# Stick-breaking attention as a sum over differenced values, and half of its gates as paired half-size products

## The chip, the cores and the metric

The kernel runs on one core of a Trainium2 chip. The metric is the device time of one execution in microseconds. TensorE (PE) does the matrix products and the transposes, VectorE (DVE), ScalarE (ACT) and GpSimd (POOL) the elementwise work, and SyncE (SP) issues all the DMAs that matter here, in order, from one queue. Weight loads of TensorE have a row of their own in the profile, PEld.

## The reference, cut to what matters

One layer of a decoder: `h = RMSNorm(x)`, one input projection of `h`, a gated linear attention branch (GLA, 4 heads), a stick-breaking branch (8 heads of width 128), learned merge gates, and an output projection. T = D = 1024. The part that the change rewrites:

```python
z = q @ k.T * scale                      # per head, 128 queries against their causal prefix
log1m = where(causal, log_sigmoid(-z), 0)
between = cumsum(log1m, reverse=True) - log1m
A = where(causal, exp(log_sigmoid(z) + between), 0)
o_sb = A @ v                             # then times silu(s_gate), then @ w_pb
```

So the weight of key s for query t is beta[t,s] times the product of (1 - beta[t,j]) over the keys j between s and t.

## The kernel before

Every matrix product is done in float32r with operands split into a high and a low part, hi and lo, and three matmuls (hi*hi, hi*lo, lo*hi). A split is one ACT copy (L165) and one DVE subtraction (L166). The stages, in order:

- **Norm and first values.** `x` is normed, transposed and split. The products in token-major form (`proj_n`, L223) give the stick-breaking values of heads 0 and 1 together with the rank-16 decay code, and then the values of the other heads (`vjobs`, `v_unit`). They need no transpose: the tokens already lie on the partitions. `store_v` writes them to DRAM (`d_v`).
- **Pairs.** Most other projections are done 256 columns at a time by `pair_job`, a Strassen-Winograd scheme: 7 units, each a product of half size (12 matmuls of 128x512, L270 to L272), in place of 8. Its weights need four sums on POOL (L244 to L247) and seven split halves. A list, `Pairs([...])`, sets the order of 28 pairs: merge gates, GLA values (`gv_pair`, which transposes its result on PE, L605), GLA q, k and gates, stick-breaking q and k, merge gates. Units run one by one between other work: 22 beside the GLA decay, some beside jobs that load and sum weights for later (`tjobs`), `GLA_AT` = 56 units in all before GLA begins, and then 4 for each block of GLA.
- **Stick-breaking.** 8 heads times 8 query blocks are 64 steps. Step s issues `scores` for step s+2, then filler, then `turn` for step s. `scores` does the z products (L956 to L958), one or two pieces in two PSUM banks; on each piece ACT makes two sigmoids, of -z into `eb` (L960) and of z into `be` (L961); DVE runs a scan of products over the whole row of `eb` (L964); POOL puts zeros into the last 128 columns of `be` above the diagonal (L965); DVE multiplies `be` by the shifted scan (L968). `turn` transposes the 1 to 8 blocks of `be` on PE (L980) and splits them into `ath`, `atl` (the four blocks of the same half) and `afh`, `afl` (the four far blocks). `values` (matmuls L1001 to L1003 into `av`) runs twice per head, after the turns of step 0 (second half of the head before) and step 4, multiplies by the gate (L1004) and stores `d_osb`.
- **Filler.** The eight stick-breaking gates (L204 to L206, 24 matmuls of 128x512 in a unit, two units for each head, then SiLU) and the GLA output projection run as single units between these steps. `SB_PLAN` says how many units stand before and after the turn of each of a head's steps: one at step 3, one at step 6, one after step 7. Two units run before the loop and six after it.
- **q loads.** `load_q` (L903) loads the queries of two steps at a time into one of two buffers, in turn; the load for steps 4 and 5 of a head goes into the buffer that steps 0 and 1 read, so it can start only when the z product of step 1 has read it.
- **Output.** Both projections of the stick-breaking output and of the merged result, again as pairs of half-size products, then the residual and the norm.

From GLA to the end of stick-breaking the order on every engine comes from the framework's scheduler, which works on the order in which the code is written; each engine then runs its own list in order.

## Time and profile before

| | us |
|---|---|
| three runs | 1201.83, 1204.47, 1204.98; median 1204.47 |
| the profiled execution, its own time | 1205.73 |
| its span, first to last instruction | 1204.0 |
| norm and first values (0 to 115) | 115 |
| pairs beside decay, weight sums and GLA (115 to 727) | 612 |
| stick-breaking with filler (727 to 1015) | 288 |
| output (1015 to 1204) | 189 |

The times of stages are read off the span by where their lines first appear. In a busy row, overlapping matmuls count once; the start of one matmul to the start of the next is the rate at which PE works.

### The profile page before, as it was taken

Reading aid. Unit: us, or ns where it says so; the run is one execution under the profiler, and the core shown is the slowest. Engines: PE = TensorE matmul, PEld = TensorE weight load, DVE = VectorE, ACT = ScalarE, POOL = GpSimd, SP = SyncE. Lnnn points to the kernel's source line nnn. Section 1 sums busy time; section 2 is a strip of 40 time slices with the busy share of each in tenths; the row PEclk is TensorE's granted clock in tenths of the full one; section 3 lists DMA queues with packets and bytes.
Section 4 is the critical chain, followed back from the end, with each engine's and each line's share of the span. In section 5 each row is a group of like instructions: output and inputs, shape, how many; then the busy total and the mean of one; then the engine's idle time right before and its main releaser. Section 6 shows DMA issues by size and latency. Waiting matters only on the chain.

```text
span 1204.0 us, 17310 instructions
## 1 busy us (share of the span) xinstructions
PE 1185.2 (98%) x6087; PEld 997.8 (83%) x6087; DVE 855.4 (71%) x1341; ACT 555.8 (46%) x1081; POOL 316.7 (26%) x303
## 2 busy tenths in 40 slices
PE   8999999999999999999999999999999999999997
PEld 8999878888888888888888887888878888788886
DVE  5475876896676676776674646777787775578986
ACT  5343763334334444444443425445455553365543
POOL 1486513243322322422323201111021110700001
PEclk9999999999999999999999999999999999999999
DMA  7545349988546646666655267564788547758652
GB/s 282 182 140 154 136 164 337 338 303 265 185 145 197 179 157 210 209 200 204 218 172 166 80 230 259 168 209 159 251 263 304 169 131 242 254 161 282 225 192 105
DMA packets 207090, 247.67 MB, mean 206 GB/s; under 512 B 12662, under 2 KB 141708, under 8 KB 205468
## 3 DMA queue, kind: packets, MB, share of 16 engines
q1 hardware_dynamic: 206428, 245.52, 62.3%
q8 instruction: 48, 0.79, 0.3%
q10 hardware_dynamic: 576, 1.05, 0.2%
q14 instruction: 38, 0.31, 0.1%
HBM read 154.25 MB, written 92.27 MB: 205 GB/s over the span
## 4 chain that ended last, share of the span: by engine, by line
PE 83%; DVE 7%; DMA 3%; ACT 3%; issue 3%; SPq 1%; POOL 0%; DVEq 0%; ACTq 0%
PE pp L270 12%; PE pp L272 12%; PE pp L271 12%; PE pp L223 8%; PE pp L204 4%; PE pp L206 4%; PE pp L205 4%; PE av L1002 2%; PE av L1003 1%; PE z L956 1%; PE av L1001 1%; PE tr L980 1%; PE xb L1368 1%; PE xb L1367 1%; PE z L957 1%
## 5 line engine op out<-in xcount | busy, mean ns | idle before, releaser
L166 DVE TENSOR_TENSOR wl<-tt,wh 128x1024 fp32r<-128x1024 f32 x56 | 70.6, 1261 | 49.6 <-ACT wh L165 49.4
L965 POOL TENSOR_SCALAR_AFFINE_SELECT be<-be 128x128 f32<-128x128 f32 x64 | 38.0, 595 | 236.7 <-ACT be L961 218.3
L309 DVE TENSOR_TENSOR f<-pp,f 128x512 f32<-128x512 f32 x84 | 57.8, 688 | 59.1 <-PE pp L272 55.7
L964 DVE TENSOR_TENSOR_SCAN eb<-eb,m 128x128 f32<-128x128 f32 (+3 forms) x64 | 86.7, 1356 | 9.7 <-ACT eb L960 9.5
L165 ACT ACTIVATE wh<-tt 128x1024 fp32r<-128x1024 f32 x56 | 59.3, 1059 | 67.2 <-PE pp L271 63.8
L244 POOL TENSOR_TENSOR tt<-raw 128x512 f32<-128x512 f32 x28 | 39.5, 1412 | 190.9 <-DVE wl L166 184.2
L165 ACT ACTIVATE wh<-raw 128x1024 fp32r<-128x1024 f32 x47 | 49.7, 1059 | 81.0 <-PE pp L271 39.1
L276 ACT ACTIVATE f<-pp 128x512 f32<-128x512 f32 x84 | 49.7, 592 | 79.9 <-PE pp L272 79.9
L166 DVE TENSOR_TENSOR wl<-raw,wh 128x1024 fp32r<-128x1024 f32 x47 | 70.5, 1501 | 22.4 <-ACT wh L165 21.6
L231 POOL TENSOR_TENSOR r<-r,nhalf 128x1 f32<-128x1 f32 x40 | 24.2, 604 | 193.2 <-DVE r L230 182.7
L960 ACT ACTIVATE eb<-z 128x384 f32<-128x384 f32 (+4 forms) x96 | 48.8, 508 | 43.4 <-issue 22.8
L968 DVE TENSOR_TENSOR be<-be,eb 128x128 f32<-128x128 f32 (+3 forms) x64 | 48.3, 757 | 3.6
L961 ACT ACTIVATE be<-z 128x384 f32<-128x384 f32 (+4 forms) x96 | 49.2, 513 | 0.0
L270 PE MATMUL pp<-ha22h,wh 128*128 128x512 f32 x112 | 44.7, 399 | 0.3 <-DVE f L309 0.2
L270 PE MATMUL pp<-ha11h,wh 128*128 128x512 f32 x112 | 44.5, 397 | 0.0
L270 PE MATMUL pp<-ha12h,wh 128*128 128x512 f32 x112 | 44.5, 397 | 0.0
L270 PE MATMUL pp<-S1h,wh 128*128 128x512 f32 x112 | 44.4, 396 | 0.0
L270 PE MATMUL pp<-S3h,wh 128*128 128x512 f32 x112 | 44.1, 394 | 0.0
L270 PE MATMUL pp<-S2h,wh 128*128 128x512 f32 x112 | 44.0, 392 | 0.0
L270 PE MATMUL pp<-S4h,dh 128*128 128x512 f32 x112 | 43.9, 392 | 0.0
L271 PE MATMUL pp<-ha22l,wh 128*128 128x512 f32 x112 | 43.7, 390 | 0.0
L272 PE MATMUL pp<-ha22h,wl 128*128 128x512 f32 x112 | 43.7, 390 | 0.0
(519 smaller groups left out, 3979.7 us busy)
## 6 DMA issues: line engine op xcount, KB each, us to landing
raw<-in_w_in_dram SPq DMA_DIRECT2D x31, 1024.0 KB, 6.5
d_v<-o SPq DMA_DIRECT2D x32, 256.0 KB, 3.0
d_gv<-o SPq DMA_DIRECT2D x32, 256.0 KB, 4.0
d_t<-t SPq DMA_DIRECT2D x16, 512.0 KB, 4.7
v<-d_gv SPq DMA_DIRECT2D x32, 256.0 KB, 3.5
d_ogl<-o SPq DMA_DIRECT2D x64, 128.0 KB, 2.8
d_q<-o SPq DMA_DIRECT2D x16, 512.0 KB, 5.2
d_k<-o SPq DMA_DIRECT2D x16, 512.0 KB, 3.4
```

What stands on the lines that cost most here:

```text
L165: nc.scalar.activation(hi, src, AF.Copy)
L166: eng.tensor_sub(lo, src, hi.bitcast(F32))
L223: nc.tensor.matmul(pt[:, 0:n], *ops[kb][i], start=k == 0, stop=k == 3 * KB - 1)
L270: nc.tensor.matmul(pt, bh[:, j], ah[:, j], start=first and j == 0, stop=False, skip_group_check=True)
L271: nc.tensor.matmul(pt, bh[:, j], al[:, j], start=False, stop=False, skip_group_check=True)
L272: nc.tensor.matmul(pt, bl[:, j], ah[:, j], start=False, stop=j == 3, skip_group_check=True)
L276: nc.scalar.activation(t[nm], t[bank], AF.Copy)
L309: nc.vector.tensor_add(add, bank, add)
L960: nc.scalar.activation(om[:, osl], zt[:, 0:w], AF.Sigmoid, scale=-inv_sqrt)
L961: nc.scalar.activation(be[:, osl], zt[:, 0:w], AF.Sigmoid, scale=inv_sqrt)
L964: nc.vector.tensor_tensor_scan(rest, rest, m1[:, off:T][:, ::-1], 1.0, op0=ALU.mult, op1=ALU.max)
L968: nc.vector.tensor_mul(be[:, off:T], be[:, off:T], om[:, off + 1:T + 1])
```

## The change

- The values are summed by parts. With C[t,s] the product of (1 - beta[t,j]) over j from s to t-1, the weight of key s is C[t,s+1] - C[t,s]. So the output is a sum over C[t,s] times (v[s-1] - v[s]), with -v[0] for s = 0, plus the last value row of the query block's prefix (there the masked part of the scan is 1 and the differences telescope). The scan's own output is transposed: the second sigmoid, POOL's mask and the DVE product are gone. `be` now names the scan's buffer.
- The stick-breaking values must be differenced along tokens, so they move to pairs (`sv_pair`, d-major, tokens along the free axis): `vend` keeps every 128th value column (a [128,4] copy), `diff` subtracts neighbours (a [128,511] subtraction and one column), and the result is transposed on PE, split and stored. The GLA values take their place in the token-major form.
- `values` adds `vend` and multiplies by the gate in four instructions of 128 columns in place of one of 512. It stands earlier than the turn of step 2 (second half of the head before) and of step 5.
- The gates of heads 0 to 3 become two pairs (`sg_pair`), so there are 30 pairs; 70 units in place of 56 run before GLA, and the jobs beside them start every 5 units, not every 3. Eight gate units leave the stick-breaking filler; `SB_PLAN` has one unit at step 3 and one at step 6.

```diff
-SB_PLAN = [(0, 0), (0, 0), (0, 0), (1, 0), (0, 0), (0, 0), (1, 0), (0, 1)]
+SB_PLAN = [0, 0, 0, 1, 0, 0, 1, 0]
-GLA_AT = 56
+GLA_AT = 70
...
+    def sg_pair(i):
+        return pair_job(w_in, C_SG + i * DV,
+                        lambda J, n, bank, add: silu(total(bank, add), d_sg[2 * i + J][:, half(n)]))
+    def sv_pair(i):
+        held = []
...
+            h = 2 * i + J
+            nc.vector.tensor_copy(vend[:, h, 4 * n:4 * n + 4], add[:, P - 1:HALF:P])
+            held.append((J, n, h, add))
+            if (J, n) != (1, 1):
+                while held:
+                    diff(*held.pop())
+        def diff(J, n, h, add):
+            d = ev.tile([P, HALF], F32, tag="f", name="f")
+            nc.vector.tensor_sub(d[:, 1:HALF], add[:, 0:HALF - 1], add[:, 1:HALF])
+            if n:
+                nc.vector.tensor_sub(d[:, 0:1], vend[:, h, 3:4], add[:, 0:1])
+            else:
+                nc.vector.tensor_scalar(d[:, 0:1], add[:, 0:1], -1.0, None, op0=ALU.mult)
...
-                  [gv_pair(0)] + gla_qk(0) + [gg_pair(0), gv_pair(1), gg_pair(1)] + gla_qk(1) +
-                  [gv_pair(2), gg_pair(2), gv_pair(3), gg_pair(3)] +
-                  [f for i in range(4) for f in (qk_pair(C_SQ, i, d_q), qk_pair(C_SK, i, d_k))] +
-                  [merge_pair(C_MB, i, d_gb) for i in range(4)] + [merge_pair(C_MA, 3, d_ga)], late)
+                  gla_qk(0) + [gg_pair(0), gg_pair(1)] + gla_qk(1) + [gg_pair(2), gg_pair(3)] +
+                  [f for i in range(4) for f in (qk_pair(C_SQ, i, d_q), sv_pair(i), qk_pair(C_SK, i, d_k))] +
+                  [sg_pair(i) for i in range(2)] + [merge_pair(C_MB, i, d_gb) for i in range(4)] + [merge_pair(C_MA, 3, d_ga)], late)
...
-            nc.scalar.activation(om[:, osl], zt[:, 0:w], AF.Sigmoid, scale=-inv_sqrt)
-            nc.scalar.activation(be[:, osl], zt[:, 0:w], AF.Sigmoid, scale=inv_sqrt)
+            nc.scalar.activation(om[:, off + pc * w:off + (pc + 1) * w], zt[:, 0:w], AF.Sigmoid, scale=-inv_sqrt)
...
-        nc.gpsimd.affine_select(be[:, T - P:T], be[:, T - P:T], pattern=[[-1, P]],
-        nc.vector.tensor_mul(be[:, off:T], be[:, off:T], om[:, off + 1:T + 1])
...
-        nc.vector.tensor_mul(gate, pav, gate)
+        for q in range(4):
+            cs = slice(q * P, (q + 1) * P)
+            nc.vector.scalar_tensor_tensor(gate[:, cs], pav[:, cs], vend[:, h, 4 * g + q:4 * g + q + 1], gate[:, cs],
+                                           op0=ALU.add, op1=ALU.mult)
...
-        st.run(SB_PLAN[i][0])
+        st.run(SB_PLAN[i])
+        if i == 2 and h:
+            values(h - 1, 1)
+        elif i == 5:
+            values(h, 0)
         turn(h, i)
-        st.run(SB_PLAN[i][1])
-        if i % 4 == 0 and s:
-            values(*((h, 0) if i else (h - 1, 1)))
```

The order on the engines changes with it. First PE at the passage from head 0 to head 1, in the kernel before: the last `values` matmuls, the rest of step 3's z product, the turn of step 1 and the first z product of step 4 (128x320):

```order
L1001 MATMUL av<-ath,v 128x256
L1002 MATMUL av<-atl,v 128x256
L1003 MATMUL av<-ath,v 128x256
L957 MATMUL z<-k,q 128x512
L958 MATMUL z<-k,q 128x512
L980 MATMUL tr<-ident,be 128x128 x2
L956 MATMUL z<-k,q 128x320
```

The same passage in the changed kernel, from the turn of step 7 that follows the z product of step 1, to the first z product of step 4:

```order
L988 MATMUL tr<-ident,be 128x128 x4
L988 MATMUL pp<-ident,be 128x128 x4
L970 MATMUL z<-k,q 128x384
L971 MATMUL z<-k,q 128x384
L972 MATMUL z<-k,q 128x384
L988 MATMUL tr<-ident,be 128x128
L970 MATMUL z<-k,q 128x512
L971 MATMUL z<-k,q 128x512
L972 MATMUL z<-k,q 128x512
L1009 MATMUL av<-afh,v 128x512
L988 MATMUL tr<-ident,be 128x128 x2
L970 MATMUL z<-k,q 128x320
```

A filler unit and a whole `values` stood between the z products of steps 1 and 4; now the unit is gone and all of `values` but one matmul stands behind.

Second, DVE inside a pair whose result is transposed. Before, the end of `gv_pair(2)`: a total (`f<-pp,f`), a weight split of the next pair (`dl`, `wl`), and the low parts of the transposed result (`o<-tr,o`):

```order
L309 TENSOR_TENSOR f<-pp,f 128x512
L166 TENSOR_TENSOR dl<-raw,dh 128x512
L166 TENSOR_TENSOR o<-tr,o 128x512
L166 TENSOR_TENSOR wl<-tt,wh 128x1024
L166 TENSOR_TENSOR o<-tr,o 128x512 x2
```

Now the end of the first `sv_pair`, units 4 to 6:

```order
L609 COPY vend<-f 128x4
L308 TENSOR_TENSOR f<-pp,f 128x512
L165 TENSOR_TENSOR dl<-raw,dh 128x512
L609 COPY vend<-f 128x4
L617 TENSOR_TENSOR f<-f 128x511
L621 TENSOR_SCALAR f<-f 128x1
L617 TENSOR_TENSOR f<-f 128x511
L619 TENSOR_TENSOR f<-vend,f 128x1
L165 TENSOR_TENSOR wl<-tt,wh 128x1024
```

Two differences with their edge columns now stand between a total and the transposes that read them, and two results are transposed together (`tr<-ident,f` x8 on PE).

## Rows read from the trace of the kernel before

**Rows 1.** Page, part 1: busy time, share, instructions; part 2: granted clock

```profile
PE 1185.2 (98%) x6087; PEld 997.8 (83%) x6087; DVE 855.4 (71%) x1341; ACT 555.8 (46%) x1081; POOL 316.7 (26%) x303
PEclk9999999999999999999999999999999999999999
```

**Rows 2.** Windows: stretch, busy us of PE, PEld, DVE, ACT, POOL, clock, DMA share, GB/s

```profile
115.00:265.00 150.00, 149.49 (x669) 121.92 (x668) 117.81 (x128) 74.48 (x95) 54.37 (x35) 1.00 0.73 248
265.00:727.00 462.00, 462.00 (x2285) 380.42 (x2284) 305.02 (x627) 199.19 (x419) 135.23 (x130) 1.00 0.61 191
727.00:1015.00 288.00, 282.51 (x1481) 238.75 (x1480) 217.54 (x280) 145.16 (x330) 38.05 (x64) 1.00 0.64 210
```

**Rows 3.** Timeline of PE inside a gate unit: start us, duration us, line, operation

```profile
822.89 0.39 PE L206 MATMUL pp<-ha21h,wl 128*128 128x512 f32 x1
823.12 0.39 PE L204 MATMUL pp<-ha22h,wh 128*128 128x512 f32 x1
823.34 0.39 PE L205 MATMUL pp<-ha22l,wh 128*128 128x512 f32 x1
823.57 0.39 PE L206 MATMUL pp<-ha22h,wl 128*128 128x512 f32 x1
```

**Rows 4.** Waits 727 to 1015, PE and PEld: total us, times, longest us

```profile
PE av L1002 <- DVE atl L166: 3.1, 3, 1.5
PE z L956 <- ACT be L961: 1.6, 4, 0.7
PE pp L980 <- DVE be L968: 0.4, 1, 0.4
PE tr L980 <- DVE be L968: 0.3, 1, 0.3
...
PEld z L956 <- ACT be L961: 6.8, 17, 1.0
PEld av L1002 <- DVE atl L166: 4.5, 5, 1.8
PEld tr L980 <- DVE be L968: 1.0, 2, 0.7
```

**Rows 5.** Groups by line, 727 to 1015: busy us, mean ns, idle before

```profile
L968 DVE TENSOR_TENSOR be<-be,eb 128x128 f32<-128x128 f32 (+3 forms) x64 | 48.3, 757 | 3.6
L1004 DVE TENSOR_TENSOR f<-av,f 128x512 f32<-128x512 f32 x16 | 11.0, 686 | 17.0 <-PE av L1003 17.0
L570 DVE TENSOR_TENSOR o<-pp,o 128x512 f32<-128x512 f32 x15 | 10.3, 687 | 11.0 <-ACT o L569 6.3 <-DMA raw<-in_w_in_dram 4.8
L166 DVE TENSOR_TENSOR wl<-raw,wh 128x1024 fp32r<-128x1024 f32 x13 | 15.9, 1224 | 15.1 <-ACT wh L165 14.9
...
L961 ACT ACTIVATE be<-z 128x384 f32<-128x384 f32 (+4 forms) x96 | 49.2, 513 | 0.0
```

**Rows 6.** Groups by line and shape, whole span: the nearest to the new DVE work

```profile
L309 DVE TENSOR_TENSOR f<-pp,f 128x512 f32<-128x512 f32 x84 | 57.8, 688 | 59.1 <-PE pp L272 55.7 <-issue 2.1 <-PE tr L854 1.0
L166 DVE TENSOR_TENSOR o<-f,o 128x512 fp32r<-128x512 f32 x24 | 19.6, 816 | 4.7 <-ACT o L165 4.1
L166 DVE TENSOR_TENSOR dl<-raw,dh 128x512 fp32r<-128x512 f32 x28 | 20.2, 722 | 5.3 <-ACT dh L165 5.3
L857 DVE SCALAR_TENSOR_TENSOR g<-tr,vcol,g 128x128 f32<-128x128 f32 x64 | 19.4, 344 | 20.1 <-PE tr L854 20.1
L230 DVE TENSOR_SCALAR r<-ssq 128x1 f32<-128x1 f32 x40 | 5.8, 146 | 6.8 <-ACT xs L389 6.1 <-ACT on L844 0.7
```

**Rows 7.** Timeline of PE at a passage between heads, step 1's z to step 4's

```profile
826.16 0.28 PE L958 MATMUL z<-k,q 128*128 128x256 f32 x1
826.28 0.60 PE L980 MATMUL tr<-ident,be 128*128 128x128 f32 x4
826.72 0.60 PE L980 MATMUL pp<-ident,be 128*128 128x128 f32 x4
827.08 0.42 PE L956 MATMUL z<-k,q 128*128 128x384 f32 x1
827.34 0.33 PE L957 MATMUL z<-k,q 128*128 128x384 f32 x1
827.50 0.34 PE L958 MATMUL z<-k,q 128*128 128x384 f32 x1
...
839.35 0.39 PE L956 MATMUL z<-k,q 128*128 128x320 f32 x1
```

**Rows 8.** Timeline of SP there, and the tile q, 727 to 1015: landing

```profile
820.61 0.42 SPq L893 DMA_DIRECT2D k<-d_k  x1
826.48 0.52 SPq L903 DMA_DIRECT2D q<-d_q  x1
...
DMA to landing us min/median/max: 3.0/3.6/6.5
```

More of the change, by code (lines that the diff above doesn't have):

```diff
@@ L346, in hybrid_layer @@
     vst = {}
+    vend = const.tile([P, SB_H, NT], F32, tag="vend", name="vend")
     def store_v(key, i, tb):
-        st = vst.pop((key, tb // 2)) if tb % 2 else None
-        if st is not None:
-            for e in range(2):
-                nc.sync.dma_start(d_v[2 * i + e][:, tb - 1:tb + 1], st[:, :, :, e * P:(e + 1) * P].bitcast(F32))
+        if tb % 2:
+            nc.sync.dma_start(d_gv[i][:, tb - 1:tb + 1], vst.pop((key, tb // 2)).bitcast(F32))
     def v_stage(key, tb):
@@ L379, in load_vr @@
             rows = w_in[4 * i * P:(4 * i + 4) * P, :]
-            nc.sync.dma_start(raw[:, :, 0:DV], rows[:, C_SV:C_SV + DV].rearrange("(k p) c -> p k c", p=P))
+            nc.sync.dma_start(raw[:, :, 0:DV], rows[:, C_GV:C_GV + DV].rearrange("(k p) c -> p k c", p=P))
             nc.sync.dma_start(raw[:, :, DV:VR], rows[:, C_GR:C_GR + RANK].rearrange("(k p) c -> p k c", p=P))
@@ L482, in hybrid_layer @@
     ebl = const.tile([P, GLA_H, NCH], F32, tag="ebl", name="ebl")
-    vjobs = [(i, C_SV + i * DV) for i in range(1, SB_H // 2)]
+    vjobs = [(i, C_GV + i * DV) for i in range(1, GLA_H)]
     v_load(vjobs[0][1], vjobs[0][0])
@@ L591, in merge_gate @@
         nc.scalar.activation(o, o, AF.Sigmoid, bias=vcol[:, b0 + eb:b0 + eb + 1])
-    def gv_pair(h):
+    def sg_pair(i):
[3 more added lines that the diff above has]
+        held = []
         def evict(J, n, bank, add):
@@ L604, in turn @@
                 for b in range(4):
-                    nc.tensor.transpose(pt[:, b * P:(b + 1) * P], add[:, b * P:(b + 1) * P], ident)
+                    nc.tensor.transpose(pt[:, b * P:(b + 1) * P], d[:, b * P:(b + 1) * P], ident)
                 o = stage()
                 split(pt, o[:, 0], o[:, 1])
-                for i in range(2):
-                    nc.sync.dma_start(d_gv[h][:, 4 * n:4 * n + 4, i, J * P:(J + 1) * P],
-                                      o[:, i].bitcast(F32).rearrange("p (b c) -> p b c", c=P))
+                for e in range(2):
+                    nc.sync.dma_start(d_v[h][:, 4 * n:4 * n + 4, e],
+                                      o[:, e].bitcast(F32).rearrange("p (b c) -> p b c", c=P))
             late.append(turn)
-        return pair_job(w_in, C_GV + h * DV, evict)
+        return pair_job(w_in, C_SV + i * DV, evict)
     def gla_qk(i):
@@ L730, in hybrid_layer @@
     for k in range(8):
-        at = 3 * k
+        at = 5 * k
         for i in range(2):
@@ L918, in hybrid_layer @@
     bets = {}
-    ebuf = [sb.tile([P, T + 16], F32, tag=f"eb{i}", name=f"eb{i}", bufs=1) for i in range(2)]
     m1 = sb.tile([P, T], F32, tag="m1", name="m1", bufs=1)
@@ L924, in hybrid_layer @@
                             base=0, channel_multiplier=1)
-    for e in ebuf:
-        nc.gpsimd.memset(e[:, T:T + 1], 1.0)
-    bets["first"] = sb.tile([P, T], F32, tag="be", name="be", bufs=3)
     wraw = raw_tile()
@@ L944, in scores @@
         off = T - L
-        om = ebuf[i % 2]
-        be = bets.pop("first", None)
-        if be is None:
-            be = sb.tile([P, T], F32, tag="be", name="be", bufs=3)
-        bets[h, i] = be
+        om = bets[h, i] = sb.tile([P, T], F32, tag="be", name="be", bufs=4)
         npc = 1 if L <= HALF else 2
@@ L1072, in o_dma @@
         return (go, False)
-    line = [gate_load(0), gate_load(1)]
-    for h in range(5):
-        line += [gate_load(h + 2), gate(h, 0), gate(h, 1)]
+    line = [gate_load(4), gate_load(5), gate_load(6), gate(4, 0), gate(4, 1)]
     line += [gate(5, 0), gate_load(7), gate(6, 0), gate(7, 0), o_dma(0), gate(5, 1), pa_load(0), gate(6, 1), pa_load(1),
```

3 lines of the change are left out of this document (removed).

## The prediction, made before the changed kernel ran

> **What bounds the kernel now.** I read the page's busy times first: PE is busy for 98% of the span, DVE for 71%, ACT for 46%, POOL for 26%, and TensorE's granted clock is in the top tenth in every slice [rows 1]. A busy PE may still be a waiting one, so the next view is the table of windows, which tells where it has gaps: between 265 and 727 none, in the stick-breaking stage (727 to 1015) 5.5 us of 288 [rows 2]. Then PE's timeline, for the rate: inside a unit the starts of 128x512 matmuls are 0.23 apart, 0.75 us for three steps between the first and the last of the four rows [rows 3]; over the long runs of such units the step is 0.227, and I use that. So PE works at one steady rate, and a matmul that is taken out is worth its 0.227 us wherever nothing else is late. Last, the table of waits for the stick-breaking stage [rows 4]. It is the only stage in which PE is held up more than a few tenths, by two things that the change touches: the second sigmoid `be`, which keeps a z bank, and the split `atl`, for which `values` waits because it stands right behind the turn.
>
> The sum is made against the profiled execution: own time 1205.73, span 1204.0, so 1.73 lies around the span. The median of the three runs is 1204.47, 1.26 lower; I carry differences over to the median unchanged.
>
> **Matmuls.** Four gates were 4 x 48 = 192 matmuls of 128x512 and become 2 x 84 = 168. The number of values pairs equals that of GLA values pairs before (four, with 16 times four transposes in both), and the token-major products have the same shapes. Net: 24 matmuls fewer, 24 x 0.227 = **-5.45**. Of this, eight units (43.6) leave the stick-breaking stage and 14 pair units (38.1) are put ahead of GLA, beside weight jobs that are now spread wider; in the pair stages PE ran with at most 0.5 us of gaps in 150 and with none in 462 [rows 2], so I charge nothing for the place. If the DMA share there (0.73) rose enough to delay a weight load, each late load would show as a PE gap.
>
> The Trainium skill, "Perfetto Trace Analysis", section Identifying the Most-Contended Engine, says that matmul busy time is no good measure of how near TensorE is to its limit and that the busy share of weight loads is to be read instead. That share is 83% [rows 1], so by the rule PE would have a sixth in hand and the 24 matmuls could be worth less, at the least nothing: the whole sum would then be -1.7. The steady step between starts decides for me, since no gap is left in it.
>
> **Work taken off ACT, POOL and DVE in the stick-breaking stage.** ACT loses 49.2, DVE the product, 48.3 [rows 5], POOL 64 masks, its only work in that window, 38.05 [rows 2]. DVE gains the four-part `values`: 64 x 0.344 (nearest row: a scalar-tensor-tensor of 128x128 from PSUM [rows 6]) less 11.0 [rows 5] = +11.0; eight SiLU products less at 0.687 and four weight splits less at 1.22 [rows 5] are -10.4. DVE comes to 217.5 - 48.3 + 11.0 - 10.4 = 170 in a stage of about 242, 70% where it was 76%. None of this is on PE's path by itself, so it counts zero; what it brings is in the next term. It is also why two filler units for each head, not three, can be enough: DVE's need falls by more than the filler's cover.
>
> **Old waits.** In the stage PE's own idle time is 5.4 (3.1 + 1.6 + 0.4 + 0.3), and the weight loads' idle time is 12.5 in the three rows shown (6.8 + 4.5 + 1.0) [rows 4]; the second includes time that a running matmul covers, the first leaves out slips too small to show as idle. The truth lies between. For the z banks I take the middle of 1.6 and 6.8, 4.2, for `values` the middle of 3.1 and 4.5, 3.8. The first go because a bank is free after one sigmoid; the second because `values` now stands one or two steps behind the splits that it reads. What is late next is the scan: a turn still waits for it, and the next head's first turns come closer together. So I count three quarters of 8.0: **-6.0**, with bounds 0 and -8.0.
>
> **A new wait between heads.** This is the cost that the diff hides. The load of queries for steps 4 and 5 goes into the buffer that step 1's z product reads. In the trace PE leaves that product at 826.28, SP issues the load at 826.48, and PE needs it at 839.35, 13 us later [rows 7, 8]: a filler unit and a whole `values` lie between. In the changed order at the passage from head 0 to head 1 there lie only ten transposes more (eight, then two) and one of step 2, three matmuls of 384, three of 512 and one of `values`: 0.80 for the eight, 0.5, 0.11, 0.68, 0.23 and 0.22 by the spacings of [rows 3, 7], 2.6 us. Counted the same way the other six passages have 3.5, 14.8, 3.5, 3.3, 3.3 and 3.3. The load needs 0.2 + 3.6 = 3.8 at the median landing [rows 8]. PE then waits 1.2 + 0.3 + 0 + 0.3 + 3 x 0.5 = **+3.3**. With the shortest landing, 3.0, it is 0.6; with the longest, 6.5, at all six, 20.7. I take the median, since most loads in that window land near it.
>
> [...]
>
> **Differences in the pairs.** Per half of a head: a [128,4] copy, a subtraction of 511 and one column, DVE 0.146 + 0.816 + 0.146 by the nearest rows [rows 6], 16 times, 17.7 us where DVE has 157 free of 462 [rows 2]. On the path stands only the end of a pair. After unit 5, DVE does a total, the `dl` split, a copy and two differences with their columns: 0.69 + 0.72 + 0.15 + 2 x 0.97 = 3.5, while PE has unit 6, 12 x 0.227, and the first four of eight transposes, 0.44, together 3.2. The second four wait 0.3, four times; one of the four pairs has a GLA block there that covers it. **+1.0**; 0 if DVE's place is ahead, 6.4 if a weight split of 1.22 stands in front each time. DVE's waits for PE at the totals, 55.7 us in all [rows 6], say that it is usually in time.
>
> **The sum.** -5.45 - 6.0 + 3.3 + 1.0 = -7.15: span 1196.9, own time 1198.6, and for the median 1204.47 - 7.15 = **1197.3**.
>
> **Rivals.** (1) The query load is always in time and the old waits go entirely: -5.45 - 8.0 = -13.4, 1191.0. For it: the transposes between heads may themselves be held by DVE, which delays PE and hides the load. Against it: one passage is more than 1 us short at the median landing. (2) Slower: the query loads between heads. If they land in 6.5 at all six passages, the sum is -5.45 - 6.0 + 20.7 + 1.0 = +10.2, 1214.7. It decides the sign once the six waits make more than 10.5, 1.7 each, a landing of 4.8. Against it: the median of 3.6; for it, SP is one queue in order, and the load of a whole head's k goes out 6 us earlier [rows 8]. (3) The change does not free PE: the old waits come back as waits for the scan, because the turns stand closer. Then -5.45 + 3.3 + 1.0 = -1.2, 1203.3, no change that can be told. The rule on weight loads above would give nearly this time by another way, the saved matmuls being worth nothing. For it: the waits of `values` and of the turns in [rows 4] are waits for DVE already. Against it: DVE's share falls.
>
> **How the numbers follow.** Chances: the forecast 0.50 (its own range 1193 to 1201), rival 1 0.22, rival 3 0.16, rival 2 0.12. About 0.3%, 3.6 us, is what a measurement of this kernel can tell from no change: faster is below 1200.9. The forecast and rival 1 lie there, 0.72; rival 3 and the mild part of rival 2 are the same, 0.18; the rest of rival 2 is slower, 0.10. The range leaves out the best of rival 1 and most of rival 2: 1190 to 1204.5.
>
> **What would show it.** Right: 24 matmuls fewer at the same step; no wait of z for an ACT sigmoid and none of `values` for `atl`; at the first z product of step 4 (128x320) a PE gap of 0.3 to 1.2 us that ends with the landing of q, at up to six passages; a few tenths at the transposes of eight in the values pairs; a stick-breaking stage of about 242 us. Wrong: gaps of 2 us or more at the passages, gaps at turns that end with a scan, or any gap in the pair stages.

## The result: slower by 0.4%, and the profile after

The changed kernel takes 1208.1 us (median of 9 runs), the kernel before 1203.82 (9 runs): 1.0038 times as long, 95% interval 1.0028 to 1.0049. The forecast was 1197.3 with a range of 1190 to 1204.5, so it was wrong in sign and the time lies outside its range. The profiled execution of after has a span of 1206.3 and an own time of 1208.47, against 1204.0 and 1205.73; the difference between the two profiled executions is 2.7, that between the medians 4.3.

The page of after, parts 1 and 2 (answers to [rows 1]): busy time and instructions of each engine, and the granted clock in 40 slices.

```profile
PE 1181.6 (98%) x6063; PEld 995.6 (83%) x6063; DVE 833.0 (69%) x1383; ACT 533.1 (44%) x995; POOL 289.8 (24%) x245
...
PEclk9999999999999999999999999999999999999999
```

The 24 matmuls are gone (6087 to 6063), and all other engines have less to do. Nothing on this page tells that the kernel became slower. The table of windows does (answers to [rows 2]; the stages begin later now, because 14 more pair units run ahead of the GLA; columns: stretch, its length, busy us of PE, PEld, DVE, ACT, POOL, granted clock, DMA share, GB/s):

```profile
115.00:265.00 150.00, 149.66 (x660) 122.73 (x659) 112.57 (x119) 74.44 (x93) 52.69 (x35) 1.00 0.70 244
265.00:765.00 500.00, 494.68 (x2433) 406.28 (x2432) 336.77 (x704) 213.67 (x440) 146.79 (x134) 1.00 0.57 183
765.00:1015.00 250.00, 241.85 (x1287) 206.07 (x1286) 166.00 (x247) 105.29 (x221) 0.00 (x0) 0.99 0.68 229
```

PE has 5.3 us of gaps in the pair stage, where it had none before, and 8.15 in the stick-breaking stage, where it had 5.5. The clock, 1.00 there before, is 0.99. Who is waited for stands in the table of waits of after (answers to [rows 4]; total us, times, longest), first from 265 to 767, then from 767 to 1016:

```profile
PE tr L626 <- DVE o L165: 4.0, 3, 1.9
PE tr L874 <- DVE o L165: 0.7, 1, 0.7
PE tr L626 <- DVE f L621: 0.6, 1, 0.6
```

```profile
PE z L970 <- DMA q<-d_q: 2.8, 3, 1.6
PE z L970 <- ACT be L973: 2.2, 1, 2.2
PE pp L203 <- DVE o L1055: 0.9, 1, 0.9
PE pp L203 <- DVE o L569: 0.8, 1, 0.8
PE av L1009 <- ACT ath L164: 0.7, 1, 0.7
...
```

L626 is the turn (the transposes) of a differenced values result, L970 the z product. So there are two new costs in two stages: turns that wait for DVE at the ends of the values pairs, and z products that wait for queries. A third wait, 2.2 for an ACT sigmoid, stands at 949. Measured from the start of one matmul to the start of the next, less the steady step of its shape, the gaps over 0.3 us are 6.1 us in the pair stage (1.22, 0.88, 2.10, 0.73 and 1.18, at 375.7, 445.8, 517.0, 569.8 and 587.6), and 9.9 in the stick-breaking stage (7.6 before).

**The queries.** The timeline of SP and PE at the passage from head 2 to head 3 in after (start, duration, engine, line; a bracket is the idle time and its end):

```profile
863.09 0.33 SPq L916 DMA_DIRECT2D v<-d_v  x1
863.47 0.43 SPq L1081 DMA_DIRECT2D oa22l<-d_ogl  x1
863.95 0.52 SPq L923 DMA_DIRECT2D q<-d_q  x1
```

```profile
872.17 0.28 PE L1011 MATMUL av<-ath,v 128*128 128x256 f32 x1
874.09 0.60 PE L970 MATMUL z<-k,q 128*128 128x320 f32 x1 [1.64 <-DMA q<-d_q]
```

The buffer of the load issued at 863.95 was free at 855.72, when step 1's z product had ended. SP, one queue in order, issued the load 8.2 us later: the loads of `oa` stand ahead of it, and the load of `v` at 863.09, which waits until `values` has read the buffer it goes to. The table of SP's waits from 850 to 867:

```profile
...
SPq L916 <- PE av L1011: 3.5, 1, 3.5
...
```

The kernel before had the same hold. At its passage from head 3 to head 4 step 1's z product ended at 860.88, the load of `v` waited 7.2 us for `values`, and q went out 10.6 us late:

```profile
870.66 0.33 SPq L896 DMA_DIRECT2D v<-d_v  x1
...
871.51 0.52 SPq L903 DMA_DIRECT2D q<-d_q  x1
```

It landed 4.9 us later, 0.9 ahead of the product that needed it (877.32). At the next passage q was 11.7 us late and landed 0.6 ahead. So the slack there was nearly used up before the change; the prediction read its issue from a passage where nothing stood ahead [rows 8].

In the changed kernel the load of q landed after 10.1 us, beside `v` and a megabyte for each `oa`: the row of 872 to 874 below has the DMA share at 1.06 and 411 GB/s. At the other passages the load goes out 0.03 to 0.9 us after the buffer is free, and the first z product of step 4 follows the landing by 0.04 to 1.6 us in six of the seven passages (at the last one the landing isn't recorded): little or nothing is left of the slack. The tile q's landings in that stage, which were 3.0/3.6/6.5 before [rows 8]:

```profile
DMA to landing us min/median/max: 2.9/4.3/10.1
```

**The clock.** The windows of after behind the two longest waits (same columns as above):

```profile
872.00:874.00 2.00, 0.45 (x4) 0.25 (x2) 0.00 (x0) 0.00 (x0) 0.00 (x0) 1.00 1.06 411
874.00:876.00 2.00, 1.91 (x7) 1.92 (x8) 0.00 (x0) 0.44 (x1) 0.00 (x0) 0.54 0.95 357
876.00:877.50 1.50, 1.50 (x7) 1.50 (x6) 0.98 (x1) 0.71 (x2) 0.00 (x0) 0.50 0.09 33
...
949.00:951.50 2.50, 0.36 (x3) 0.04 (x1) 1.12 (x1) 2.50 (x6) 0.00 (x0) 1.00 0.80 263
...
952.50:956.50 4.00, 4.00 (x15) 3.37 (x14) 4.00 (x7) 1.92 (x5) 0.00 (x0) 0.57 0.79 243
```

After PE had stood, the granted clock is 0.50, the lower of its two levels (1.2 GHz), while PE shows as busy. That is time lost that no column of busy time and no wait shows. An estimate, each stretch times what its clock lacks of 1.00: 2 x 0.46 + 1.5 x 0.50 = 1.7 us at the first place and 4 x 0.43 = 1.7 at the second. The first stand ends with a load of q, the second with the ACT sigmoid. In the kernel before no stretch of this stage has a clock below 1.00.

**The turns.** DVE at the end of the first values pair of after, then POOL:

```profile
373.44 1.23 DVE L165 TENSOR_TENSOR wl<-tt,wh 128x1024 fp32r<-128x1024 f32 x1 [0.95 <-ACT wh L164]
374.58 0.16 DVE L609 COPY vend<-f 128x4 f32<-128x4 f32 x1
374.65 0.68 DVE L617 TENSOR_TENSOR f<-f 128x511 f32<-128x511 f32 x1
375.25 1.23 DVE L619 TENSOR_TENSOR f<-vend,f 128x1 f32<-128x1 f32 x1
376.41 1.27 DVE L165 TENSOR_TENSOR o<-tr,o 128x512 fp32r<-128x512 f32 x2
```

```profile
374.74 1.73 POOL L243 TENSOR_TENSOR tt<-raw 128x512 f32<-128x512 f32 x1 [8.60 <-DVE wl L165]
376.43 1.27 POOL L245 TENSOR_TENSOR tt<-raw 128x512 f32<-128x512 f32 x1
```

PE's turn of this result begins when the first of the two low splits `o` is done:

```profile
377.15 0.55 PE L626 MATMUL tr<-ident,f 128*128 128x128 f32 x3 [1.06 <-DVE o L165]
```

The edge column L619, a subtraction of one column with two inputs in SBUF, takes 1.23 us. It does so in all four pairs at this place, and 0.15 in the four other instances; in the four slow ones it ends within 0.02 us of the end of POOL's pair sum L243. That sum starts here because it waits for the split `wl`, the very instruction that stands ahead of the differences.

### The profile page after: what moved, and what is told of

Same layout as the page of the kernel before. It is cut to its first block, busy times and chain, and to the rows that moved or that the text cites. A ratio compares the mean times of both kernels' runs of the same rounds, so it can differ in the third digit from the quotient of the medians.

```text
span 1206.3 us, 17004 instructions
## 1 busy us (share of the span) xinstructions
PE 1181.6 (98%) x6063; PEld 995.6 (83%) x6063; DVE 833.0 (69%) x1383; ACT 533.1 (44%) x995; POOL 289.8 (24%) x245
## 4 chain that ended last, share of the span: by engine, by line
PE 85%; DVE 6%; DMA 3%; ACT 3%; issue 2%; POOL 1%; SPq 0%; ACTq 0%; DVEq 0%
PE pp L269 14%; PE pp L270 14%; PE pp L271 14%; PE pp L222 8%; PE pp L203 3%; PE pp L204 3%; PE pp L205 3%; DMA q<-d_q 1%; PE av L1011 1%; PE av L1009 1%; PE av L1010 1%; PE z L970 1%; PE xb L1378 1%; PE xb L1376 1%; PE xb L1377 1%
## 5 line engine op out<-in xcount | busy, mean ns | idle before, releaser
L165 DVE TENSOR_TENSOR wl<-tt,wh 128x1024 fp32r<-128x1024 f32 x60 | 74.5, 1242 | 54.6 <-ACT wh L164 54.4
L308 DVE TENSOR_TENSOR f<-pp,f 128x512 f32<-128x512 f32 x90 | 61.9, 688 | 69.5 <-PE pp L271 63.6
L243 POOL TENSOR_TENSOR tt<-raw 128x512 f32<-128x512 f32 x30 | 44.3, 1478 | 234.2 <-DVE wl L165 215.6
L976 DVE TENSOR_TENSOR_SCAN be<-be,m 128x128 f32<-128x128 f32 (+3 forms) x64 | 86.2, 1349 | 13.0 <-ACT be L973 12.9
L164 ACT ACTIVATE wh<-tt 128x1024 fp32r<-128x1024 f32 x60 | 63.5, 1058 | 70.8 <-PE pp L270 68.9
L1161 POOL TENSOR_TENSOR N<-A,A 128x512 f32<-128x512 f32 x4 | 6.6, 1644 | 271.6 <-DMA A<-d_osb 271.6
L230 POOL TENSOR_TENSOR r<-r,nhalf 128x1 f32<-128x1 f32 x40 | 24.7, 617 | 192.4 <-DVE r L229 189.3
L164 ACT ACTIVATE ath<-tr 128x128 fp32r<-128x128 f32 (+1 forms) x64 | 28.3, 442 | 61.9 <-PE tr L988 61.9
L271 PE MATMUL pp<-ha11h,wl 128*128 128x512 f32 x120 | 46.9, 391 | 0.0
L271 PE MATMUL pp<-ha12h,wl 128*128 128x512 f32 x120 | 46.9, 390 | 0.0
L270 PE MATMUL pp<-ha11l,wh 128*128 128x512 f32 x120 | 46.8, 390 | 0.0
```

Of the source, the lines that this page charges most:

```text
L164: nc.scalar.activation(hi, src, AF.Copy)
L165: eng.tensor_sub(lo, src, hi.bitcast(F32))
L243: nc.gpsimd.tensor_sub(t1, b[:, 0, 1], b[:, 0, 0])
L270: nc.tensor.matmul(pt, bh[:, j], al[:, j], start=False, stop=False, skip_group_check=True)
L271: nc.tensor.matmul(pt, bl[:, j], ah[:, j], start=False, stop=j == 3, skip_group_check=True)
L308: nc.vector.tensor_add(add, bank, add)
```

## The experiments

Each run is timed against the kernel before on the same chip. The medians of before there were 1203.46 (e1 to e4), 1203.25 (e5 to e8), 1204.47 (e9 to e12) and 1203.40 us (e13, e14). The ratios in the text are to these.

| run | what it is | median us | ratio to before, 95% |
|---|---|---|---|
| (after) | the change | 1208.1 | 1.0028 to 1.0049 |
| e1 | after, third difference behind the turns | 1208.67 | 1.0033 to 1.0070 |
| e2 | after, edge columns and `vend` on ACT | 1203.72 | 0.9992 to 1.0010 |
| e3 | after, four q buffers, loads earlier | 1197.66 | 0.9944 to 0.9968 |
| e4 | after, d_ga one unit earlier | 1211.12 | 1.0050 to 1.0074 |
| e5 | summation by parts alone, three units | 1209.08 | 1.0030 to 1.0057 |
| e6 | before, third q buffer | 1202.51 | 0.9985 to 1.0003 |
| e7 | after, third q buffer | 1197.63 | 0.9939 to 0.9963 |
| e8 | e3 and e2 together | 1194.19 | 0.9906 to 0.9933 |
| e9 | after, k and v loaded later | 1208.58 | 1.0015 to 1.0047 |
| e10 | e8 and d_ga earlier | 1195.94 | 0.9911 to 0.9938 |
| e11 | paired gates alone, third q buffer | 1194.37 | 0.9903 to 0.9931 |
| e12 | e8 and q2 on DVE | 1191.30 | 0.9876 to 0.9903 |
| e13 | paired gates alone, two q buffers | 1204.80 | 0.9999 to 1.0020 |
| e14 | e5 with four q buffers | 1209.46 | 1.0039 to 1.0063 |

### Which step of the turns is late: e1, e2, e12

e1, in the values pair's `evict`, with the third result's `diff` called behind the turns that are due:

```
-            if (J, n) != (1, 1):
+            if (J, n) == (0, 1):
+                post.append(lambda a=held.pop(): diff(*a))
+            elif (J, n) != (1, 1):
```

> Edit: in a values pair the difference of the last result, (0,1), is written behind the transposes of the two results before it, so that on DVE the two low splits of the tr banks stand ahead of the third 511-column subtraction and its edge column; everything is still computed. Theory A (two tr banks wait for DVE, which does the third difference first, 0.68 + 1.23 us at 374.65 to 376.48): the five gaps of PE in the pair stage, 1.22 + 0.88 + 2.10 + 0.73 + 1.18 = 6.1 us, shrink to under 1.5 in sum; time 1208.1 - 5 = 1203. Rival (the third transposes wait for their own operand, the difference, which now comes later by the two splits, 1.4 us): the gaps stay, with f as the releaser, and the time is 1207 to 1209.

The theory fell and the rival held: 1208.67, with gaps of 1.34, 0.78, 2.09, 0.74 and 1.23 us at the same places. The waits, 320 to 721, now name the transposes' own operand (L625 is the edge column, L632 the turn in this kernel):

```profile
PE tr L632 <- DVE f L625: 4.2, 3, 1.9
```

With the two low splits ahead, the edge column comes that much later. Whichever of them stands last, DVE is late as a whole; the first reading, that the order of DVE holds two `tr` banks, took the last releaser for the cause.

e2:

```
-            nc.vector.tensor_copy(vend[:, h, 4*n:4*n+4], add[:, P-1:HALF:P])
+            nc.scalar.activation(vend[:, h, 4*n:4*n+4], add[:, P-1:HALF:P], AF.Copy)
...
-                nc.vector.tensor_sub(d[:, 0:1], vend[:, h, 3:4], add[:, 0:1])
+                nc.scalar.activation(d[:, 0:1], add[:, 0:1], AF.Identity, scale=-1.0, bias=vend[:, h, 3:4])
...
-                nc.vector.tensor_scalar(d[:, 0:1], add[:, 0:1], -1.0, None, op0=ALU.mult)
+                nc.scalar.activation(d[:, 0:1], add[:, 0:1], AF.Copy, scale=-1.0)
```

> Edit: the copies of the last columns (vend) and the one-column differences at the edges go from DVE to ACT; the 511-column subtraction stays on DVE, in the order of the changed kernel. Theory A1 (the edge column costs DVE 1.23 us in place of 0.15 wherever a pair sum of POOL runs beside it, four times, and vend 1.0 us twice, just where two tr banks wait): DVE is quicker by 1.2 to 2.2 us at the end of each values pair, the five gaps of 6.1 us fall to 1.5 or less, time 1204 or below. Rival (it is the work as a whole, 0.68 us of subtraction and the order): the gaps fall by only the 0.15 us of each small instruction, time 1207 to 1208.5. If what waits is ACT's copy of the third result, an ACT that has more to do makes it worse: 1209 or above.

1203.72, 4.4 less than after. Three of the five gaps are gone; 2.03 and 0.69 are left. DVE at the first values pair in e2:

```profile
373.35 1.23 DVE L165 TENSOR_TENSOR wl<-tt,wh 128x1024 fp32r<-128x1024 f32 x1 [1.15 <-ACT wh L164]
374.49 0.68 DVE L617 TENSOR_TENSOR f<-f 128x511 f32<-128x511 f32 x1
375.09 1.28 DVE L165 TENSOR_TENSOR o<-tr,o 128x512 fp32r<-128x512 f32 x2
```

The low splits start 1.3 us earlier than in after, at 375.09 for 376.41. So it was the small instructions, copies and columns together. The place where 2.03 us are left shows the same thing on other instructions; DVE of e2, then POOL:

```profile
512.12 2.06 DVE L165 TENSOR_TENSOR wl<-tt,wh 128x1024 fp32r<-128x1024 f32 x1
...
514.31 1.78 DVE L617 TENSOR_TENSOR f<-f 128x511 f32<-128x511 f32 x1
```

```profile
511.82 1.28 POOL L801 TENSOR_TENSOR q<-qe,fac 128x512 f32<-128x512 f32 x1 [1.53 <-DVE qsl L165]
514.26 1.28 POOL L243 TENSOR_TENSOR tt<-raw 128x512 f32<-128x512 f32 x1 [1.16 <-DVE wl L165]
```

POOL's product for a GLA half, L801, and its pair sum started 0.30 and 0.05 us ahead of a DVE instruction with two inputs, and these took 2.06 in place of 1.23 and 1.78 in place of 0.68. e12 takes that product from POOL, on top of e8:

```
-        nc.gpsimd.tensor_mul(ch3(q2), ch3(qe),
+        nc.vector.tensor_mul(ch3(q2), ch3(qe),
```

> Edit: both cures, and the product q2 of a GLA half (eight in all, 1.28 to 2.62 us each on POOL) goes to DVE; PE's order is the same row for row. Theory A2 (POOL beside DVE stretches DVE's instructions: at 512 to 516 us the split wl takes 2.06 in place of 1.21 and the subtraction 1.78 in place of 0.68 while q2 and a pair sum run on POOL): the last stall of 2.0 us of a values pair goes, 1194.2 - 2 = 1192.2. Rival (DVE is late there by its own work, and eight more products of some 0.7 us make it later): 1194 to 1198.

1191.30, 2.9 less than e8 (3.6 by the ratios to before), with PE's order the same row for row. The gap of 2.0 is gone; 0.69 is left of the five. DVE got more work and PE got it sooner.

### Is it the load of queries: e3, e7, e6, e9

e3 gives steps 4 to 7 two buffers of their own and issues every load two steps earlier; e7 only adds a third buffer, with the loads where they were; e6 does that in the kernel before.

```
e3-        tag = "d" + "hl"[m % 2]
e3+        t = (sw.tile(..., tag="d" + "hl"[m], bufs=1) if m < 2 else sb.tile(..., tag="q"))
e3-            h2, i2 = steps[s + 4]
e3+            h2, i2 = steps[s + 6]

e6, e7-    tag = "d" + "hl"[m % 2]
e6, e7+    i = (4 * h + m) % 3
e6, e7+    t = (sw.tile(..., tag="d" + "hl"[i], bufs=1) if i < 2 else sb.tile(..., tag="q", bufs=1))
```

> Edit: the queries of steps 4 to 7 get two buffers of their own, and every load of queries is issued two steps earlier; nothing else moves. Theory B (a late load of q makes PE wait 1.8 us at 872.17 and some tenths at two other products, and behind the wait the granted clock is 0.50 from 874.3 to 877.5, which costs 1.8 us more): the waits of z for DMA (2.8 us in three) go, the clock at the first passage stays at 1.00, time 1208.1 - 2.8 - 1.8 = 1203.5. Rival (at that passage something else is late by as much, the splits for values, 0.9 + 0.5 us at 869 to 870, or DVE): the clock falls there anyway, and the time is 1206 to 1208.

> Edit: the changed kernel with a third buffer for queries, the three used in turn; loads at the same place in the program, not two steps earlier. Theory B1 (the buffer is what the load waits for, 3.5 to 6.9 us before the product that needs it): all but the passage from head 2 to 3 is cured, where SP holds the load back 8.2 us behind the loads of v and of oa; 1198 to 1201. Rival B2 (the place in SP's queue and the crowded DMA decide, an early issue is needed): 1204 or above.

> Edit: the kernel before with a third buffer for queries, the three used in turn; loads at the same place in the program. Theory B (the wait for q is new: before, 6.7 to 16.7 us lie between the last reader of a buffer and the next product that needs it, more than a landing of 3.0 to 6.5): no change, 1202.5 to 1204.5. Rival (q is short in both kernels, the wait is only seen as another one before): faster by 4 or more, 1199.5.

1197.66 and 1197.63 in after, more than twice the gain that was expected of e3, and 1202.51 in before, no change that can be told. The waits of PE in e3 from 765 to 1020:

```profile
PE z L970 <- ACT be L973: 1.2, 1, 1.2
PE av L1009 <- ACT afh L164: 0.4, 1, 0.4
PE tr L988 <- DVE atl L165: 0.2, 1, 0.2
```

The waits for q are gone, and so are those for `o`, `ath` and `atl` that no theory had put down to it. The gaps over 0.3 us fall from 9.9 to 2.7 (-7.2), and the two stretches at half clock are gone (-3.4): 10.6 by the trace, 10.4 by the medians. Of the 7.2 only some 3 were waits for the load. Another 3.5 (0.99, 1.40 and 1.09, at 827, 869 to 870 and 882) were waits of other work near these passages: filler matmuls for `o` on DVE and `values` for its splits. Of the 3.4 for the clock, half lies behind the stand at 949, which falls from 2.3 to 1.4 us. With more buffers the scheduler orders 85 of PE's 6063 rows otherwise, in e3 as in e7. What the load costs by itself and what the other order costs can't be told apart by these runs, because the order follows from the buffers.

e7 against e3 says that the buffer is the cause, and not where the load stands in the program. e6 says that the wait is new: in the kernel before 6.7 to 16.7 us lie between the last reader of a buffer and the product that needs the next load.

e9 issues the next head's k and v two steps later:

```
-        if i == 1 and h + 1 < SB_H:
+        if i == 3 and h + 1 < SB_H:
             load_head(h + 1)
```

> Edit: the changed kernel with the load of the next head's k and v issued two steps later (step 3, not step 1), behind the loads of queries of the passage, so that on SP no load of q stands behind a load of v that waits for the values product. PE's order moves in four rows only. Theory B2 (SP's queue: at the passage from head 2 to 3 the load of q is issued 8.2 us after its buffer is free, behind v, and lands beside 4 MB of oa): that passage no longer waits, its 0.9 + 0.5 + 1.8 us of gaps and the half clock behind it (1.8) go, 1203.5 to 1205; at the other passages, where the load goes out 0.03 us after its buffer is free, nothing changes. Rival B1 (the two buffers alone): 1207 to 1209.

No change, 1208.58. SP in e9 at the same passage:

```profile
863.80 0.33 SPq L916 DMA_DIRECT2D v<-d_v  x1
864.18 0.43 SPq L1081 DMA_DIRECT2D oa22l<-d_ogl  x1
864.66 1.96 SPq L923 DMA_DIRECT2D q<-d_q  x2
```

The edit missed its aim: the `v` that waits for `values` is the second half of the head that has just begun, and two steps later in the program its load still stands ahead of q. It waits 3.2 us here; q goes out 8.2 us after its buffer is free (856.42) and lands after 10.0. So this run says nothing on what the place on SP is worth; e7 says that a third buffer makes it matter no more.

### The sigmoid that waits for d_ga: e4, e10

At 949 PE stands for 2.3 us: a z product waits until ACT's sigmoid `be` has read its bank, and that stands on ACT behind the sigmoid of a merge gate `o`, which waits for the load of d_ga. ACT of after there:

```profile
941.56 0.27 ACT L973 ACTIVATE be<-z 128x128 f32<-128x128 f32 x1
948.68 0.72 ACT L590 ACTIVATE o<-o,vcol 128x512 f32<-128x512 f32 x1 [6.85 <-DMA o<-d_ga]
949.31 1.04 ACT L164 ACTIVATE wh<-raw 128x1024 fp32r<-128x1024 f32 x1
```

e4 issues that load one filler unit earlier; e10 does so on top of e8.

```
-        merge_gate(o[:, 0], d_ga, 0, eb, n)
+        o = ga.pop((eb, n))
+        nc.scalar.activation(o[:, 0], o[:, 0], AF.Sigmoid, bias=vcol[:, eb:eb + 1])
...
+    line.insert(at, ga_load(*pas[u]))
```

> Edit: the load of d_ga for a product with w_pa is issued one filler unit earlier than the product; nothing else moves. Theory C (the sigmoid of d_ga waits on ACT for its load, 6.85 us at 948.68, and four evictions that PE waits for are queued behind it; PE stands 2.34 + 0.37 us and then runs at half clock until 956.4, 1.8 us): the gap at 949 goes, time 1208.1 - 4.5 = 1203.6. Rival (the weight split of 1.04 us behind the sigmoid, or DVE's 2.3 us scan, holds the same products): PE still waits a microsecond or more for ACT there and the time is 1206.5 to 1208.5.

> Edit: both cures (four buffers for queries, edge columns on ACT) and the load of d_ga one filler unit earlier. Theory C (alone, the earlier d_ga cost 3.0, because it stood ahead of loads of q that were late already; with q in time it only takes away the 1.25 + 0.37 us at the sigmoid that waits for d_ga): 1194.2 - 1.6 = 1192.6. Rival (the earlier load is harmful or useless of itself): 1194 to 1197.

Both failed. e4 is slower than after by 3.0: the gap at this place falls only to 1.5, and PE now waits longer for queries (the waits of e4, 765 to 1020):

```profile
PE z L970 <- DMA q<-d_q: 6.3, 3, 2.3
PE z L970 <- ACT be L973: 1.3, 1, 1.3
```

With the queries cured it does no such harm but no good either (1195.94, with the interval of e8's ratio overlapping its own), and the gap of 1.2 stays. The edit missed its aim there: on SP the load of d_ga stands right behind a store of `d_osb`, 0.37 us after it, in e4 and e10 (933.17 and 933.54 in e10) as in after (943.50 and 943.87). One unit earlier in the program it still goes out only when that store can. So these runs don't say what an earlier load would be worth; what makes PE stand at 949 is the late d_ga by the waits alone, not shown by a cure.

### Which half of the change costs: e5, e11, e13, e14

e5 is after without its paired gates: the eight gates are 16 filler units again, three units a head.

```
-                  [sg_pair(i) for i in range(2)] + [merge_pair(...)
+                  [merge_pair(...)
...
-SB_PLAN = [0, 0, 0, 1, 0, 0, 1, 0]
+SB_PLAN = [0, 0, 0, 1, 0, 0, 1, 1]
...
-GLA_AT = 70
+GLA_AT = 56
```

> Edit: the changed kernel without its paired gates. Summation by parts and its values pairs stay; all eight gates are again 16 filler units in the stick-breaking stage, with three units a head (the third at step 7, which lies between the first z products of the next head and its step 4); the GLA begins 14 pair units earlier, as in the kernel before. 24 matmuls more than the changed kernel, 5.45 us. Theory B (the passages between heads are too short for the load of q; own buffers were worth 10.4): the third unit covers the load by itself, nearly all of the 10.4 comes back, 1208.1 + 5.45 - 9 = 1204.5, and PE's z waits for no DMA. Rival (the loss is in the summation by parts itself, its four-part values and fewer sigmoids, and q was one of several late things): the waits of about 10 us stay and the time is 1211 or more.

1209.08, between what the two forecast; PE still waits 1.8 us for q, and 3.0 us at the last `values`. e14 is e5 with e3's buffers:

> Edit: the changed kernel without its paired gates (eight gates as filler units, three a head), with four buffers for queries loaded two steps earlier. 24 matmuls more than the changed kernel with that cure (1197.7). Theory (summation by parts by itself pays in the stick-breaking stage about what its differences cost in the pair stage): 1197.7 + 5.45 = 1203, no change against the kernel before. Rival (with three units DVE had time enough, and only the cost of the differences is left): 1206 to 1210, as without the cure (1209.1).

1209.46, as the rival has it. With three units the queries cost nothing that can be told, and the summation by parts is slower than the kernel before by 6.1. Its waits of PE from 765 to 1020 are one line,

```profile
PE av L1009 <- ACT afh L164: 4.6, 2, 2.9
```

the last `values` of the stage and one before it, behind which the clock falls once more (0.66 in the window 1010 to 1015); the gaps at the transposes of the pair stage are there too, six of 5.8 us together, and two more of 1.3 and 1.4 at 224 and 231, where a product waits for a result of the pair ahead.

e11 and e13 are the other half: the kernel before with four gates as two pairs and two units a head, with a third q buffer (e11) and with the two of before (e13).

```
+    def sg_pair(i):
+        return pair_job(w_in, C_SG + i * DV, lambda J, n, bank, add: silu(...))
...
-SB_PLAN = [(0, 0), ..., (1, 0), (0, 1)]
+SB_PLAN = [(0, 0), ..., (1, 0), (0, 0)]
...
-GLA_AT = 56
+GLA_AT = 70
```

> Edit: the kernel before with the other half of the change alone, four gates as two pairs and two filler units a head, and a third buffer for queries (worth 0 to 0.9 in the kernel before); stick-breaking with two sigmoids, mask and product as before. Theory (the summation by parts is what lets two units suffice: DVE has some 207 us of work in a stage that would be 240, 86%, and ACT 49 us more): the waits for be and atl grow by more than the 5.45 us of matmuls saved, 1204 to 1212. Rival (two units are enough without it, and the summation by parts brought nothing): 1197 to 1199.

> Edit: the kernel before with the paired gates and two filler units a head alone, two query buffers as before. In the order of PE's instructions the passages between heads shrink from 12.5 to 16.4 us of work (6 of them) to 2.6, 3.8, 14.3, 7.5, 3.1, 3.1, 3.1, much as in the changed kernel. Theory F (the unit taken out uncovers the load of q): PE waits for q at several passages, and the time is 1200 to 1206, 6 to 11 above the same kernel with a third buffer (1194.4). Rival S (it is the summation by parts, by its moved values products and its loads): no wait for q, 1194 to 1197.

e11 takes 1194.37, by 3.3 faster than the whole change with the same buffer (e7; 4.1 by the ratios to before). The theory, that only the summation by parts lets two units suffice, fell. The windows of e11, and under them the second window of e7:

```profile
265.00:765.00 500.00, 500.00 (x2452) 411.72 (x2451) 327.31 (x658) 214.25 (x441) 146.16 (x136) 1.00 0.59 187
765.00:1002.00 237.00, 234.89 (x1264) 197.76 (x1263) 203.35 (x265) 136.24 (x316) 26.95 (x64) 1.00 0.72 234
```

```profile
765.00:1002.00 237.00, 235.21 (x1274) 200.69 (x1273) 165.81 (x247) 105.34 (x222) 0.00 (x0) 1.00 0.70 237
```

DVE is busy for 203 of 237 us in e11 and for 166 in e7, ACT for 136 and 105; PE for 234.9 and 235.2. That looks as if the 37 us taken off DVE bought PE 0.3, but these columns don't show all that PE loses. From the first z product to the last `values` matmul, with the same matmuls to do, PE takes 235.9 us in e11 and 233.1 in e7 (232.4 in e3, 232.3 in e12; 243.3 in after). So in this stage the summation by parts is worth some 3 us. In the pair stage e11 has no gap at all, and there e7 loses more than that.

e13 takes 1204.80, 10.4 more than e11 for one buffer of 2 KB a partition less. The waits of PE in e13, 765 to 1020:

```profile
PE z L961 <- DMA q<-d_q: 3.7, 4, 2.8
PE tr L985 <- DVE be L973: 1.9, 3, 0.9
...
```

So the wait for q belongs to the filler unit that was taken out of each head, not to the summation by parts: most of the passages without that unit have only a few microseconds of work in either kernel.

### Both cures: e8

> Edit: both cures together, the four buffers for queries with loads two steps earlier, and the edge columns and vend on ACT. The two theories concern different stages (pair stage and stick-breaking), so the gains add: 1197.7 - 4.4 = 1193.3, better than the kernel before by 10. Rival (one of them was noise or gives back in the other stage): 1196 or above.

1194.19: the gains add. With e12 the changed kernel takes 1191.30, 0.9889 times the kernel before (0.9876 to 0.9903), the fastest of all.

## Why the prediction was wrong, step by step

**Matmuls, -5.45: right as far as the runs go.** 24 fewer in the trace, at the same step of 0.227, and no charge for the place of the 14 pair units: 149.66 busy of 150 in the first window of after, 500.00 of 500 in e11. The weight loads' busy share is 83% before and after and named none of the things that then decided the time.

**Work taken off three engines, 0: what hung on it was wrong.** The text said that DVE's smaller share is why two units a head can be enough. e11 has two units, two sigmoids, the mask and the product, DVE at 86%, and takes 10.1 us less than the kernel before. So two units are enough without it, and DVE's 76% before [rows 2, 5] was no bound.

**Old waits, -6.0: the size is near, the reason holds for a part.** PE's waits for `atl` and `be`, 5.4 before with those for the product [rows 4], are 1.5 in e7; they are 1.8 in e11, with two sigmoids and `values` where it was, and 4.3 in e6, the kernel before with the third buffer. But smaller slips count too. From the first z product to the last `values` matmul, what PE takes above the steady steps, slips of any size together, is 19.2 us before, 17.1 in e11 and 14.2 in e7. Of these 5 us some 2 went with the third unit and the paired gates and some 3 with the summation by parts. Which part of the latter did it, the second sigmoid, the product or the place of `values`, isn't shown, and why waits go with the unit is open; a run that takes the third unit away and nothing else wasn't tried. In e14, with three units and one sigmoid, no wait for `be` or `atl` is left, but 4.6 for `afh`, so `values` can still come too early. The three rows of weight loads in this term add up to 12.3, not 12.5.

**New wait between heads, +3.3: the wait came, the size was wrong by 7.** The term measured 10.4 (e3 and e7 against after; e13 against e11). The waits of z for q alone are 2.8, close to the forecast, but not where it put them, and that is luck. At the five short passages whose landing is recorded the loads landed after 3.0 to 4.4 us, as counted, and only two of them show a gap over 0.3 (0.9 and 0.6); the passage with 14.8 us of cover, for which zero was charged, has the longest, 1.8. Three steps failed. First, the issue: at that passage SP was 8.2 us late, behind a load that waits for `values`, and the landing took 10.1. The prediction named SP as one queue in order, in its second rival, and the trace before had such holds of 10.6 and 11.7 us, but it took the issue from a passage without one [rows 8]. Second, it charged only the wait itself; behind two longer stands, this one and the one at 949, the clock fell to half, 1.7 us each. Third, it took the work around the late products as punctual; with two buffers that work was waiting itself, 3.5 us. (The spacings that it counts at the first passage add up to 2.5, not 2.6; that changes nothing.)

**Differences in the pairs, +1.0: wrong by 5.** The gaps are 6.1, near the upper bound of 6.4 (0.3 + 1.22, four times, is 6.1), which was given for another reason. The term looked at the second four of eight transposes behind unit 5; late is the third result, behind unit 6. And it took the copy and the column at 0.146 [rows 6], from an instruction of another kind: that row is a tensor-scalar with one input, which took 0.14 to 0.16 even in the seven instances beside a pair sum of POOL. The edge column has two inputs, and it took 1.22 to 1.25 just where the pair sum starts; the copies took 1.00 to 1.20 in three places. Price a small instruction by a row of its own kind.

**The sum.** With -5.45 for the matmuls, +10.4 for the queries and +6.4 for the turns (1197.66 to 1191.30 by e8 and e12), -7.05 is left over for the old waits in the +4.3 measured, where -6.0 was forecast and -8.0 was the bound. By the ratios to before the queries are worth 9.9, the turns 8.1, and the rest is -7.9; so the remainder is known to about 1 us. A part of it lies behind the stage: a gap of 1.3 us at 1036 in the kernel before, for an `o` on DVE, is gone. The two terms that were put at +3.3 and +1.0 came to +16.8, and it took both to turn the sign. The second rival had the sign and, with 10.5 as the point from which it decides, nearly the size of its cause; it stood at 0.12. Its own mechanism, landings of 6.5 at six passages, didn't come: one load was late, by the place in the queue that it named in its favour. Of the signs named beforehand as showing it wrong, gaps in the pair stages came, and 1.8 + 0.5 + 0.9 us of gaps at the worst passage, none of 2 us alone.

**The two halves.** With the queries cured, the paired gates alone are worth -10.1 against before (e11), the summation by parts alone +6.1 (e14), and both -5.6 (e7). The summation by parts pays only when its turns are cured too: e12 is 3.1 faster than e11, whose pair stage has no gap that the same cure could close.

## What to carry to other kernels

A filler unit is not only time for a slow engine; it is also the cover of every load whose buffer is freed just ahead of it. Before taking one out, list these loads with the time from the last reader to the next need, the issue at each of the places and not at one, and the landing in the most crowded stretch, and add a buffer where they come near. Price a small instruction by a row of its own kind, with as many inputs, and look at how long it takes where POOL works beside it, not at the mean. And compare stages by the time between the same two instructions: the columns of busy time hid 3 us here.

## What the runs showed of the hardware

A DVE subtraction of one column, with two inputs in SBUF, took 1.22 to 1.25 us in place of 0.15 in the four instances that started while a POOL instruction on SBUF operands ran, and ended with it. It goes both ways: the pair sum L243 that started 0.09 us behind DVE's subtraction took 1.73, the one behind it 1.27. The Trainium skill, "SBUF — State Buffer", section SBUF: two separate sides, says that whichever of a DVE instruction with two SBUF inputs and a GpSimd instruction that reads SBUF starts first has the shared ports for the whole of it, and the other one waits; these rows agree, with the cost independent of how small the waiting one is. A one-column tensor-scalar with one input (L230 before) wasn't held: 0.14 to 0.16 in the seven instances beside a pair sum of POOL. A `vend` copy of 4 columns, with one input too, took 1.00 to 1.20 in place of 0.16 in three instances and ended within 0.04 us of the end of a POOL instruction; why copies are held and this tensor-scalar isn't, no run here shows.

PE standing for 1.8 us (with 0.9 and 0.5 shortly before) and for 2.3 us was followed by a granted clock of 0.50, 1.7 us lost each time by estimate. A stand of 2.1 us, at 517 in after, was not: the clock is 1.00 from 515 to 525.
